# Masked chunk matrices of RWKV as row-tiled products per head, four chunks to one item and two banks

## The chip, the cores and the metric

The kernel runs on one core of one Trainium2 chip. The metric is device time of one launch in microseconds (us); less is better. Engines are named as the profile names them: PE is the matrix engine (TensorE), PEld its weight loads, DVE is VectorE, ACT is ScalarE, POOL is GpSimd, SP is SyncE, whose queue issues the transfers (DMA). PSUM is the memory that PE writes its products to, in eight banks of 512 fp32 columns; SBUF is the working memory of the other engines.

## The reference, cut to what matters

One layer of a hybrid decoder: one input projection, then a gated linear attention branch (GLA, 4 heads) and an RWKV-7 branch (16 heads of 64) beside each other, then a gated merge, an output projection and a layer norm. It runs over a prompt of 1024 tokens and over 8 single-token samples.

```python
p = jnp.einsum('btd,dn->btn', x, w_in)          # 1024 -> 9360 columns
...
def step(S, inp):                               # RWKV-7, every head, every token
    rt, wt, kt, vt, kkt, at = inp
    sa = jnp.einsum('bhvk,bhk->bhv', S, -kkt)
    S = S * wt[:, :, None, :] + sa[..., None] * (kkt * at)[:, :, None, :] + vt[..., None] * kt[:, :, None, :]
    y = jnp.einsum('bhvk,bhk->bhv', S, rt)
    return S, y
...
m = (jax.nn.sigmoid(gate_a) * jnp.einsum('btc,cd->btd', o_gla, w_up_gla)
     + jax.nn.sigmoid(gate_b) * jnp.einsum('btc,cd->btd', o_rwkv, w_up_rwkv))
out = jnp.einsum('btd,de->bte', m, w_out)
y_out = _layernorm(DEEPNORM_ALPHA * x + out, ln_g, ln_b, LN_EPS)
```

The kernel does the recurrence of RWKV in chunks of 64 tokens. Within a chunk it needs, for each head, four masked 64 by 64 matrices: the products of the two decayed key-side rows (b and k) with the two decayed query-side rows (a and r), one pair under a strict triangle and the other with its diagonal.

## The kernel before

The prompt is worked through in two passes of 512 tokens (`PASS`); the 8 samples ride along in the first. In each pass the projection runs over column blocks of 128: eight weight tiles, each as a high and a low part, give 24 products per block and stretch of tokens (`proj<-xh,wpart` and `proj<-xl,wpart` in the profile; `big` and `pY` banks are also lent to the up-projections and the output). The 16 RWKV heads are handled as eight pairs, one head on partitions 0 to 63 and the other on 64 to 127 (`HS`). For each pair the stream `pair` runs `front` (decays, keys, and the masked matrices), then the solution of the triangular systems with help of transfers through DRAM (`LD`, `XD`), then `back`, `turn`, `chain` (eight chunks one after the other, each with four small products: `pch<-wide,gg`, `pY<-az,wide`, `pch<-rh,XT`, `pch<-wide`, and `pY<-gg,wide`) and `norm`. GLA heads run as streams of their own (`gla_head`).

No one writes the order of the instructions by hand. All streams are Python generators that yield operations; `run` takes at each step the operation whose key is smallest: the start that the planner computes for it from its own prices (`price`) and hop times, less a bonus by kind of stream. Each operation that is yielded is one item and is issued at once to its engine's queue; each queue is then worked off in that order on the chip. So a price that changes or an operation that is longer moves the rest of the plan as well. Tiles of PSUM come from rings: `BANKS` gives `big` three banks, `proj` two, `pY` two and `pch` one. `get(tag, n)` waits until n buffers of a ring are idle at the same time, and other streams may take a single one meanwhile; `free` gives a buffer back.

The place of the change is the end of `front`. `BK` (the tile `wide`) holds for each chunk 128 columns, for the one head b and k, for the other k and b. `AZ` (the tile `az`) holds for each chunk 256 columns in the order kind, head, token. Its block for head 0 is filled on partitions 0 to 63 alone and that for head 1 on 64 to 127 alone; the rest is zero from the start. So one product over all 128 partitions per chunk gives both heads' matrices. Two chunks fill one bank, DVE multiplies the bank with the mask `gmask` into `gg`, and the bank is given back: four banks and four masks per pair.

Of the kernel before, what the change touches and what calls it, by code (L numbers as in the profile page):

```python
# [20 lines left out]
P = 128  # L21
D = 1024
# [10 lines left out]
C = 64  # L33
NCH = HT // C
# [52 lines left out]
HS = (slice(0, 64), slice(64, 128))  # L87
# [42 lines left out]
class Op:  # L130


    def __init__(self, ways, out, ins, lag=0.0, table=None, tiles=None, port=""):
        self.ways, self.out, self.ins, self.lag, self.table, self.tiles = ways, out, ins, lag, table, tiles
        self.port = port
        self.eng, self.fn, self.cost = ways[0]


def tiles(name, args):

    m = args[0].free_size()
    return tuple(32 if v <= 32 else 64 if v <= 64 else P for v in (args[0].shape[0], m))


def price(eng, name, out, args, ins):

    n = out.free_size()
    src = [x for x in ins if x.tensor.space != PSUM] if eng == "A" else ins
    if eng == "P":
        m = args[0].free_size()  # L150
        rows, cols = tiles(name, args)
        if name == "transpose":
            return 0.112
        if args[0].dtype == F32R:
            return max(m / 1200, n / 2165) if rows == cols == P else (m + n) / 1200
        if rows == cols == P:
            return 2 * max(m, n) / 1200 + 0.005
        return 2 * (m + n) / 1200 * rows * cols / P ** 2
    if eng == "S":
        return 0.56  # L160
    if eng == "A":
        extra = len(ins) - 1
        return 0.097 + n / 1200 + (0.042 if len(src) == len(ins) else 0.0) + 0.094 * extra
    wide = max([n, *(x.free_size() for x in ins)]) if name in ("tensor_reduce", "bn_stats", "bn_aggr") else n
    if eng == "V":
        if name == "tensor_tensor_scan":
            return 0.1 + n / 480
        if name in ("tensor_copy", "copy", "memset") and ins and ins[0].tensor.space != PSUM:
            wide = wide / 2
        scalars = sum(x.free_size() == 1 for x in ins[1:]) if name in ("scalar_tensor_tensor", "tensor_scalar") else 0  # L170
        return 0.068 + wide / 960 + 0.06 * scalars
    if name in ("tensor_scalar", "memset"):
        return 0.08 + n / 760
    return 0.1 + n / (300 if name == "tensor_copy" else 456)
# [25 lines left out]
def transfer(out, src):  # L200

    n = 4 * min(run_of(out), run_of(src), 512 if src.tensor.space == out.tensor.space else 1024)
    return out.nbytes() / n * (0.01 + n * 4.65e-5) / 16, 1.7 if out.tensor.space != DRAM else 1.2


class Engine:
# [3 lines left out]
    def __getattr__(self, name):  # L210
        def make(out, *args, **kw):
            ins = [x for x in (*args, *kw.values()) if isinstance(x, AP)]
            ways = []
            lag, table, part, port = 0.0, None, None, ""
            for eng, handle in self._handles.items():
                call = getattr(handle, "tensor_copy" if (eng, name) == ("V", "copy") else name)
                ways.append((eng, lambda call=call: call(out, *args, **kw), price(eng, name, out, args, ins)))  # L217
                if eng in "VG" and shared(eng, name, out, ins):
                    port += eng
            if eng == "S":  # L220
                lag = transfer(out, args[0])
            elif eng == "A" and name == "activation":
                table = SETS.get(args[1])
            elif eng == "P":
                part = tiles(name, args)
            return Op(ways, out, ins, lag, table, part, port)
        return make


class Stream:  # L230
# [8 lines left out]
class Order:  # L239
# [83 lines left out]
    def start(self, op):  # L323

        best = None
        for eng, fn, cost in op.ways:
            free, t = self.time[eng] + (SWITCH if eng == "P" and op.tiles != self.tiles else 0.0), 0.0
            for x in (op.out, *op.ins):
                at, by = self.ready.get(x.tensor.name, (0.0, None))
                if eng == "S" and by == "D" and x is op.out:  # L330
                    continue
                if by != eng:
                    at += HOP.get(by, 0.0) + (SPARE if eng == "P" and by in ("V", "A", "G") else LANDED if by == "D" else 0.0)
                elif eng != "P" and x is not op.out:
                    at += 0.13
                t = max(t, at)
            t = max(t, self.read.get(op.out.tensor.name, 0.0))
            if eng in op.port:
                free = max(free, self.port["G" if eng == "V" else "V"])
            late, t = free - t, max(t, free)  # L340
            if eng in "VA" and self.held(eng, op):
                cost += HOLD
            end = t + cost
            if len(op.ways) > 1:
                end += BIAS if eng == "V" and "A" in op.ways[0][0] else ASIDE if eng == "G" and "G" in op.port else 0.0
            if best is None or end < best[0]:
                best = end, t
                op.eng, op.fn, op.cost, op.late = eng, fn, cost, max(0.0, late)
        return best[1]
# [10 lines left out]
    def run(self):  # L360
        while self.streams:
            best, before = None, list(self.streams)
            self.urgent = self.needed()
            for s in before:
                self.advance(s)
                if s.op is not None:
                    t = self.start(s.op)
                    key = t - (s.on_pe if s.op.eng == "P" else s.prio)
                    if s.kind in self.urgent:
                        key -= URGENT  # L370
                    if s.op.table not in (None, self.table):
                        key += max(0.0, TABLE - AGE * s.op.late)
                    if best is None or key < best[0]:
                        best = key, t, s
            if best is None:
                assert self.streams != before, "streams wait for one another"
                continue
            _, t, s = best
            op, s.op = s.op, None
            cost = op.cost  # L380
            if op.table not in (None, self.table):
                cost += TABLE
                self.table = op.table
                self.nc.scalar.preload_act_table_set(self.table)  # L384
            op.fn()
            self.time[op.eng] = max(self.time[op.eng], t + cost)
            if op.eng in op.port:
                self.port[op.eng] = t + cost
            if op.eng == "P":
                self.tiles = op.tiles  # L390
            elif op.eng in "VA":
                for x, q in self.starts(op):
                    self.quads[op.eng][x is op.out, x.space] = q
            end = t + cost
            if op.eng == "S":
                self.dma = max(self.dma, end) + op.lag[0]
                end = self.dma + op.lag[1]
            end = max(end, self.ready.get(op.out.tensor.name, (0.0,))[0])
            self.ready[op.out.tensor.name] = end, "D" if op.eng == "S" else op.eng
            for x in op.ins:  # L400
                n = x.tensor.name
                self.read[n] = max(self.read.get(n, 0.0), end)


class Kern(Order):
# [654 lines left out]
    def front(self, c, p, st, d):  # L1060
        a, A, V, E = self.a, self.A, self.V, self.E
        BK_, L_ = yield from self.get("wide", 2)
        az, gg = (yield from self.get("az")), (yield from self.get("gg"))
        BK = BK_.rearrange("p (c t) -> p c t", c=NCH)
        AZ, GG = (x.rearrange("p (c k h t) -> p c k h t", c=NCH, k=2, h=2) for x in (az, gg))
# [26 lines left out]
        ps = yield from self.head_sums(te)  # L1092
# [23 lines left out]
        ps = yield from self.head_sums(te)  # L1116
# [4 lines left out]
        if c.fronts == NPAIR:  # L1121
            self.free(*c.lw)

        mk = self.cst("gmask").unsqueeze(1).to_broadcast([P, 2, 2 * P])
        for x in range(0, NCH, 2):
            p1 = yield from self.bank("big", [P, 2, 2 * P])
            for n in range(2):
                yield self.P.matmul(p1[:, n], BK[:, x + n], az[:, (x + n) * 2 * P:(x + n + 1) * 2 * P], start=True, stop=True)
            yield V.tensor_mul(gg[:, x * 2 * P:(x + 2) * 2 * P].rearrange("p (n t) -> p n t", n=2), p1, mk)
            self.free(p1)  # L1130

        NU = 4 * NCH
        LD = self.dr.tile([4, NCH, 32, 32], F32, name=f"LD{c.i}{p}")
# [27 lines left out]
        H = NCH // 2  # L1161
# [5 lines left out]
        for q in range(2):  # L1167
            b = slice(32 * q, 32 * q + 32)
            for h in range(2):
                n = 2 * q + h  # L1170
# [554 lines left out]
```

## Time and profile before

| what | value |
|---|---|
| median of 3 runs | 1603.45 us (1600.87 to 1605.56) |
| the profiled execution | 1597.82 us, of which the span of its instructions 1596.0 |
| PE busy in the span | 1550.1 us, 97% |
| PEld busy | 1371.0 us, 86% |
| DVE busy | 1282.5 us, 80% |
| ACT busy | 855.9 us, 54% |
| POOL busy | 123.5 us, 8% |
| mean DMA rate | 200 GB/s |
| mean granted clock of PE | 0.997 of full speed |

An fp32 product shows as two records on PE and two weight loads on PEld (the tile is loaded and run in two parts), an fp32r product as one of each. A row of grouped instructions reads: line, engine, operation, output <- inputs, rows*columns of the array that it uses, shape of the operand that moves through, count, then busy time in us and the mean duration of one in ns. Durations of records overlap, since the next product starts before the last has left the array; the pace of a series is therefore the distance of its starts, not the duration of one. In a timeline the first number is the start and the second the time from the first start to the last end of the merged rows, both in us.

### The profile page before, as it was taken

The numbers are of one execution on the slowest core, as the hardware profiler recorded it, in microseconds if no ns is written. First come the engines' busy times: TensorE is split into PE (matmuls) and PEld (weight loads), VectorE is DVE, ScalarE is ACT, GpSimd is POOL, SyncE is SP. The second block draws the span as 40 slices with busy tenths as digits, with TensorE's granted clock in tenths as the row PEclk, the third lists the DMA queues.
The fourth block names the chain that finished last, engine by engine and source line by source line (L and its number), as shares of the span: only waits on it lengthen the run. The fifth ranks groups of instructions, "written<-read, shape, count | busy, mean of one in ns | idle before, by whom it ended". The sixth has DMA issues, their size and how long they took to land.

```text
span 1596.0 us, 29099 instructions
## 1 busy us (share of the span) xinstructions
PE 1550.1 (97%) x9874; PEld 1371.0 (86%) x9874; DVE 1282.5 (80%) x3351; ACT 855.9 (54%) x2032; POOL 123.5 (8%) x218
## 2 busy tenths in 40 slices
PE   8999999999999999999999999999999999999998
PEld 6999999999999998787888777878777889988786
DVE  6697889878989798779788997899877786756565
ACT  5564666566657665553654464445454646544210
POOL 2011001100000011001101120011001000000000
PEclk9999999999999999999999999999999999999999
DMA  9767776676757765755465546544665467797332
GB/s 308 245 233 221 231 232 224 204 260 222 232 188 250 246 219 184 213 162 172 144 194 161 168 119 212 168 152 134 204 174 144 161 211 255 255 300 251 128 117 82
DMA packets 206641, 318.42 MB, mean 200 GB/s; under 512 B 87076, under 2 KB 102573, under 8 KB 206493
## 3 DMA queue, kind: packets, MB, share of 16 engines
q1 hardware_dynamic: 206492, 316.56, 62.6%
q8 instruction: 79, 1.29, 0.3%
q14 instruction: 70, 0.57, 0.1%
HBM read 196.82 MB, written 118.61 MB: 198 GB/s over the span
## 4 chain that ended last, share of the span: by engine, by line
PE 60%; DVE 23%; DMA 6%; SPq 4%; issue 4%; ACT 3%; POOL 0%; DVEq 0%; POOLq 0%; ACTq 0%
PE proj L217 30%; PE big L217 19%; DVE row L217 8%; PE pY L217 7%; PE pch L217 4%; SPq L217 4%; DVE Xt L217 3%; DVE X L217 3%; DVE wide L217 2%; DVE wpart L217 2%; DMA wide<-LD 1%; DVE az L217 1%; DMA wraw<-w_in 1%; ACT row L217 1%; DVE pair L217 1%
## 5 line engine op out<-in xcount | busy, mean ns | idle before, releaser
L217 PE MATMUL proj<-xh,wpart 128*128 128x256 f32 (+2 forms) x3744 | 915.5, 328 | 2.4 <-DMA wpart<-w 2.0
L217 PEld LDWEIGHTS proj<-xh,wpart 128*128 128x128 f32 x3744 | 624.2, 189 | 52.3 <-issue 5.1
L217 PE MATMUL proj<-xl,wpart 128*128 128x264 f32 (+2 forms) x1872 | 611.6, 327 | 0.9 <-DVE xl L217 0.7
L217 PEld LDWEIGHTS proj<-xl,wpart 128*128 128x128 f32 x1872 | 353.3, 189 | 25.4 <-issue 1.7
L217 ACT CAST wpart<-wraw 128x512 fp32r<-128x512 f32 x210 | 130.3, 623 | 113.7 <-PE proj L217 44.0
L217 DVE TENSOR_TENSOR wpart<-wraw,wpart 128x512 fp32r<-128x512 f32 x207 | 142.3, 689 | 38.1 <-ACT wpart L217 37.3
L217 DVE TENSOR_TENSOR row<-row 128x512 f32<-128x512 f32 (+10 forms) x302 | 164.0, 549 | 7.3 <-ACT row L217 2.4
L217 ACT ACTIVATE row<-row 128x512 f32<-128x512 f32 (+5 forms) x229 | 139.1, 611 | 36.0 <-DVE row L217 25.2
L217 DVE TENSOR_TENSOR Xt<-X,wide 128x60 f32<-128x60 f32 (+24 forms) x496 | 108.7, 219 | 17.9 <-DMA wide<-LD 6.8
L217 DVE TENSOR_TENSOR X<-X,Xt 128x60 f32<-128x60 f32 (+24 forms) x496 | 109.0, 220 | 12.3 <-DVE Xt L217 0.5
L217 ACT ACTIVATE s0p<-wide,pc 64x64 f32<-64x64 f32 x256 | 88.0, 344 | 46.7 <-DVE wide L217 41.0
L217 POOL TENSOR_TENSOR row<-row 128x256 f32<-128x256 f32 (+5 forms) x67 | 67.2, 1005 | 575.8 <-DVE row L217 238.6
L217 ACT ACTIVATE row<-proj,omu 128x256 f32<-128x256 f32 (+1 forms) x99 | 54.1, 547 | 98.6 <-PE proj L217 98.4
L217 PE MATMUL big<-row 128*128 128x128 f32 (+3 forms) x520 | 96.4, 287 | 9.4 <-DVE Xt L217 4.0
L217 PEld LDWEIGHTS big<-row 128*128 128x128 f32 (+1 forms) x520 | 74.8, 187 | 20.0 <-ACT row L217 11.3
L384 ACT ACT_TABLE_LOAD x66 | 84.7, 1283 | 1.1
L217 DVE SCALAR_TENSOR_TENSOR wide<-pch,pc,s0p 64x64 f32<-64x64 f32 x224 | 63.2, 282 | 22.7 <-PE pch L217 17.4
L217 DVE SCALAR_TENSOR_TENSOR row<-proj,pv,row 128x255 f32<-128x255 f32 (+1 forms) x99 | 56.2, 568 | 26.6 <-ACT tail L217 17.5
L217 PE MATMUL big<-xh,wpart 128*128 128x512 f32 (+2 forms) x304 | 74.8, 329 | 0.0
L217 ACT COPY row<-big 128x128 f32<-128x128 f32 (+5 forms) x134 | 38.5, 317 | 64.8 <-PE big L217 56.5
L217 PE MATMUL big<-az,wide 128*128 128x256 f32 x256 | 66.4, 384 | 0.4 <-DVE row L217 0.2
L217 PE MATMUL big<-part,headsr 128*128 128x512 f32 x128 | 55.7, 440 | 7.3 <-ACT part L217 3.4
(240 smaller groups left out, 2506.9 us busy)
## 6 DMA issues: line engine op xcount, KB each, us to landing
w<-wpart SPq DMA_DIRECT2D x146, 512.0 KB
wpart<-w SPq DMA_DIRECT2D x146, 512.0 KB
wraw<-w_in SPq DMA_DIRECT2D x146, 256.0 KB
wide<-LD SPq DMA_DIRECT2D x64, 128.0 KB
wraw<-w_up_gla SPq DMA_DIRECT2D x32, 256.0 KB
wraw<-w_up_rwkv SPq DMA_DIRECT2D x32, 256.0 KB
sg<-row SPq DMA_DIRECT2D x16, 260.0 KB
row<-sg SPq DMA_DIRECT2D x16, 260.0 KB
```

What stands on the lines that cost most here:

```text
L217: ways.append((eng, lambda call=call: call(out, *args, **kw), price(eng, name, out, args, ins)))
L384: self.nc.scalar.preload_act_table_set(self.table)
```

## The change

The masked matrices are no longer one product of 128 rows per chunk but two of 64 rows, one for each head, on the head's own partitions. The product of head h and chunk c has `BK[hs, c]` (64 x 128) as weights and moves `AZ[hs, c, :, h]` (64 x 2 x 64, two runs of 64 columns that lie 128 apart). The zero blocks of `az` are not read here any more (they still are in `chain`). Head 0 writes to one bank and head 1 to another, four chunks each, so that two `big` banks must be idle at once, and the eight products of four chunks are yielded as one item through the new function `together`: the planner places them next to each other and nothing can come between them. DVE's four masks per pair stay, with the same 512 columns each; they now write runs of 64. The planner's price of a product that uses 128 columns and fewer rows is changed, and so is that of DVE's predicated copy, which GLA uses.

```diff
@@ class Op
-        self.port = port
+        self.port, self.outs = port, [out]
@@ price
-        return 2 * (m + n) / 1200 * rows * cols / P ** 2
+        return 2 * (max(m, n) if cols == P else m + n) / 1200 * rows * cols / P ** 2 + (0.01 if cols == P else 0.0)
...
-        return 0.068 + wide / 960 + 0.06 * scalars
+        return 0.068 + wide / (480 if name == "copy_predicated" else 960) + 0.06 * scalars
@@ new
+def together(ops):
+
+    op = ops[0]
+    fns = [x.fn for x in ops]
+    op.ways = [(op.eng, lambda: [fn() for fn in fns], sum(x.cost for x in ops))]
+    op.ins = [y for x in ops for y in x.ins]
+    op.outs = [x.out for x in ops]
+    op.eng, op.fn, op.cost = op.ways[0]
+    return op
@@ start
-            for x in (op.out, *op.ins):
+            for x in (*op.outs, *op.ins):
...
-            t = max(t, self.read.get(op.out.tensor.name, 0.0))
+            t = max(t, *(self.read.get(x.tensor.name, 0.0) for x in op.outs))
@@ run
-            end = max(end, self.ready.get(op.out.tensor.name, (0.0,))[0])
-            self.ready[op.out.tensor.name] = end, "D" if op.eng == "S" else op.eng
+            for x in op.outs:
+                n = x.tensor.name
+                self.ready[n] = max(end, self.ready.get(n, (0.0,))[0]), "D" if op.eng == "S" else op.eng
@@ front
-        mk = self.cst("gmask").unsqueeze(1).to_broadcast([P, 2, 2 * P])
-        for x in range(0, NCH, 2):
-            p1 = yield from self.bank("big", [P, 2, 2 * P])
-            for n in range(2):
-                yield self.P.matmul(p1[:, n], BK[:, x + n], az[:, (x + n) * 2 * P:(x + n + 1) * 2 * P], start=True, stop=True)
-            yield V.tensor_mul(gg[:, x * 2 * P:(x + 2) * 2 * P].rearrange("p (n t) -> p n t", n=2), p1, mk)
-            self.free(p1)
+        H = NCH // 2
+        mk = self.cst("gmask").rearrange("p (k h t) -> p k h t", k=2, h=2)
+        for x in range(0, NCH, H):
+            ps = yield from self.get("big", 2)
+            ps = [y.rearrange("p (c k t) -> p c k t", c=H, k=2) for y in ps]
+            yield together([self.P.matmul(ps[h][:, n], BK[hs, x + n], AZ[hs, x + n, :, h], start=True, stop=True)
+                            for n in range(H) for h, hs in enumerate(HS)])
+            for h in range(2):
+                yield V.tensor_mul(GG[:, x:x + H, :, h], ps[h], mk[:, :, h].unsqueeze(1).to_broadcast([P, H, 2, C]))
+            self.free(*ps)
```

The first place is PE at the first pair of the first pass, around the masked matrices (`big<-az,wide`). `proj<-` rows are the projection, `big<-part,headsr` are sums over a head, `big<-row 8x512` belongs to the samples. Before:

```order
L217 MATMUL proj<-xh_235,wpart 128x256
L217 MATMUL big<-part,headsr 128x512
L217 MATMUL big<-az_167,wide 128x256 x8
L217 MATMUL big<-row 8x512
L217 MATMUL proj<-xl_273,wpart 128x256
```

And now:

```order
L217 MATMUL proj<-xh_265,wpart 128x256
L217 MATMUL big<-az_167,wide 128x128 x8
L217 MATMUL big<-row 8x512
L217 MATMUL proj<-xl_277,wpart 128x256
L217 MATMUL proj<-xh_265,wpart 128x256
L217 MATMUL proj<-xh_270,wpart 128x256
L217 MATMUL proj<-xl_298,wpart 128x256
L217 MATMUL proj<-xh_270,wpart 128x256
L217 MATMUL big<-az_167,wide 128x128 x8
L217 MATMUL proj<-xh_191,wpart 128x264
```

The eight products in one row become two items of eight, with one product of the samples and five of the projection between them.

The second place is PE at the third pair, where the chain of the pair before it (`pch` and `pY` rows) and a GLA head (`big<-row 128x1`) run beside the masked matrices. Before:

```order
L217 MATMUL pY<-az_168,wide 128x128
L217 MATMUL big<-part,headsr 128x512
L217 MATMUL proj<-xh_258,wpart 128x256
L217 MATMUL big<-az_167,wide 128x256 x2
L217 MATMUL pch<-rh,XT_172 128x128
L217 MATMUL big<-az_167,wide 128x256 x2
L217 MATMUL big<-row 128x1
L217 MATMUL big<-az_167,wide 128x256
L217 MATMUL pch<-wide 128x128
L217 MATMUL big<-az_167,wide 128x256 x3
L217 MATMUL pY<-gg,wide 128x128
```

And now:

```order
L217 MATMUL pY<-az_168,wide 128x128
L217 MATMUL big<-az_167,wide 128x128 x8
L217 MATMUL pch<-rh,XT_172 128x128
L217 MATMUL big<-row 128x1 x2
L217 MATMUL proj<-xh_223,wpart 128x256
L217 MATMUL proj<-xh_227,wpart 128x256
L217 MATMUL proj<-xl_242,wpart 128x256
L217 MATMUL proj<-xh_227,wpart 128x256
L217 MATMUL proj<-xh_235,wpart 128x256
L217 MATMUL proj<-xl_273,wpart 128x256
L217 MATMUL big<-az_167,wide 128x128 x8
L217 MATMUL pch<-wide 128x128
```

Steps of the chain stood between the masked products; now they stand before and after an item of eight. In the whole plan there are 32 such items, and at least one product of 128 rows stands between any two of them.

The third place is DVE at the same pair, where it takes the banks out through the mask (`gg<-big,cons`). `rh<-pch` and `wide<-pch,pc,s0p` are steps of the chain, `row` is GLA and the front. Before:

```order
L217 COPY rh<-pch 128x128
L217 TENSOR_SCALAR row<-row 128x256
L217 TENSOR_TENSOR row<-big,row 128x512
L217 TENSOR_TENSOR gg<-big,cons 128x512
L217 TENSOR_SCALAR row<-row,pv 128x512
L217 TENSOR_TENSOR gg<-big,cons 128x512
L217 TENSOR_SCALAR wide<-pch,pc,s0p 64x64 x2
L217 TENSOR_TENSOR gg<-big,cons 128x512 x2
```

And now:

```order
L217 COPY rh<-pch 128x128
L217 TENSOR_SCALAR row<-row 128x256
L217 TENSOR_SCALAR row<-row,pv 128x512
L217 TENSOR_TENSOR gg<-big,cons 128x8x64 x2
L217 TENSOR_SCALAR row<-row,pv 128x512
L217 TENSOR_SCALAR row<-row 128x256
L217 TENSOR_TENSOR gg<-big,cons 128x8x64
L217 TENSOR_SCALAR wide<-pch,pc,s0p 64x64 x2
L217 TENSOR_TENSOR gg<-big,cons 128x8x64
```

Four masks stay four; two of them now follow one item.

## The prediction

> **What bounds the kernel now.** I read the page first: busy times, the slices, and the shares of the chain of waits.
>
> ```profile
> span 1596.0 us, 29099 instructions
> ...
> PE 1550.1 (97%) x9874; PEld 1371.0 (86%) x9874; DVE 1282.5 (80%) x3351; ACT 855.9 (54%) x2032; POOL 123.5 (8%) x218
> ...
> PE   8999999999999999999999999999999999999998
> PEld 6999999999999998787888777878777889988786
> DVE  6697889878989798779788997899877786756565
> ...
> PE 60%; DVE 23%; DMA 6%; SPq 4%; issue 4%; ACT 3%; POOL 0%; DVEq 0%; POOLq 0%; ACTq 0%
> ```
>
> PE is full in nearly every slice and has 60% of the chain that ended last. That alone doesn't say that it works at its pace, since records overlap; so I looked at stages, and then at single products. The pairs, to which the change belongs, run from about 60 to 1260 us.
>
> ```profile
> 60.00:600.00 540.00, 531.57 (x4208) 515.32 (x4208) 469.24 (x1323) 341.35 (x888) 42.92 (x85) 1.00 0.71 230
> 600.00:1300.00 700.00, 677.75 (x3651) 562.20 (x3650) 589.33 (x1621) 368.12 (x849) 69.74 (x113) 1.00 0.56 170
> ```
>
> This view by stretches has span, then PE, PEld, DVE, ACT and POOL busy with their counts, then the granted clock (full in both). PE is busy for 98% of the first pass (531.57 of 540) and 97% of the second (677.75 of 700). DVE follows with 87% and 84%: second in line, so that a gain on PE needn't come through whole.
>
> **The products that go.** The answers for the tiles `az` and `gg`, and the timeline of the first pair:
>
> ```profile
> L217 PE MATMUL big<-az,wide x256: 377/379/483, 60.1 to 1259.2; 128*128 128x256 f32 x128
> L217 DVE TENSOR_TENSOR az<-row x61: 673/685/1737, 47.9 to 1247.2; 64x512 f32<-64x512 f32 x61
> ...
>   DVE gg L217: 7.4, 23
> ...
> L217 DVE TENSOR_TENSOR gg<-big,cons x64: 677/692/694, 61.1 to 1259.7; 128x512 f32<-128x512 f32 x64
> ```
>
> ```profile
> 59.82 3.45 PEld L217 LDWEIGHTS big<-az,wide 128*128 128x128 f32 x16
> 60.05 3.62 PE L217 MATMUL big<-az,wide 128*128 128x256 f32 x16
> ...
> 61.12 0.69 DVE L217 TENSOR_TENSOR gg<-big,cons 128x512 f32<-128x512 f32 x1 [0.17 <-PE big L217]
> ```
>
> Sixteen records of 256 columns take 3.62 us; without the duration of the last (0.38) that is 3.24 over 15 steps, 0.216 us a step. A pair has 16 records, so 16 x 0.216 = 3.46 us, and 16 pairs 55.3 us of PE. All of that goes.
>
> **The products that come.** A pair gets 16 products of 64 rows, 32 records of 128 columns, and half of 0.216 is 0.108 us for one. If two head tiles run side by side, 32 records make 16 steps of 0.108, 1.73 us a pair, and 16 pairs 27.6: PE saves 27.7 us. If they run one after the other, 32 x 0.108 is 3.46 and nothing is saved. No product with two row tiles stands in this trace. The nearest are the products of `wa`, which use 16 columns of the array each, in three tiles:
>
> ```profile
> 11.54 0.28 PE L217 MATMUL proj<-xh,wpart 128*128 128x256 f32 x1
> 11.75 1.06 PE L217 MATMUL big<-row,wa 128*16 128x256 f32 x12
> 12.74 0.39 PE L217 MATMUL proj<-xh,wpart 128*128 128x256 f32 x1
> 12.97 0.28 PE L217 MATMUL proj<-xl,wpart 128*128 128x256 f32 x1
> 13.09 0.28 PE L217 MATMUL proj<-xh,wpart 128*128 128x256 f32 x1
> ...
> 11.74 0.57 PEld L217 LDWEIGHTS big<-row,wa 128*16 128x16 f32 x12
> 12.74 0.19 PEld L217 LDWEIGHTS proj<-xh,wpart 128*128 128x128 f32 x1 [0.42 <-issue]
> ```
>
> Twelve fp32 records of about 256 columns would need 12 x 0.216 = 2.59 us in series. They take 0.99 (11.75 to 12.74), four rounds of three. So tiles of the array do run at the same time, here tiles side by side in columns; I take that for rows too.
>
> The weight loads could spoil it. They have a pace of their own:
>
> ```profile
> L217 PE MATMUL big<-Xt,L 128*128 128x32 f32 x128 | 16.6, 271 | 2.4 <-DVE Xt L217 1.7 <-ACT wpart L217 0.6
> L217 PE MATMUL big<-XT,As 128*128 128x64 f32 x128 | 16.4, 268 | 0.0
> ```
>
> Each pair has one series of eight such records. For 64 columns that is 16.4 / 16 = 1.03 us, less the last record's 0.27, over 7 steps: 0.108. For 32 columns it comes to 0.109. Half the columns aren't faster, so a load of 128 weight columns takes 0.108 a time. The new products need 32 loads instead of 16. Side by side they fit under the 16 steps; in a row they need 32 x 0.108 = 3.46 us again, the same bound as above. The Trainium skill ("TensorE: Matmul & The Clock Gate", LDWEIGHTS) speaks for the second: it says that a load costs by its columns and not by its rows, so that a half-high tile loads no faster. By that alone the change would save nothing; the same skill ("TensorEngine Tiling (Array Packing)", Key Properties) says that different tiles may load and multiply in parallel, and no run here shows either of it for row tiles. What the trace has is twelve loads of `wa` under four rounds; 16-column loads are too short to settle it. I take the parallel case as likeliest.
>
> **What a change of tiling costs.** Each item of eight is entered from a product with 128 rows and left to one: 32 times in and out. The price stands around the one kind of product with 64 rows, that of the samples:
>
> ```profile
> 46.16 0.28 PE L217 MATMUL proj<-xl,wpart 128*128 128x256 f32 x1
> 46.27 0.28 PE L217 MATMUL proj<-xh,wpart 128*128 128x256 f32 x1
> 46.48 1.02 PE L217 MATMUL big<-row 64*8 64x512 f32 x2
> 47.43 0.39 PE L217 MATMUL proj<-xh,wpart 128*128 128x256 f32 x1
> 47.66 0.28 PE L217 MATMUL proj<-xl,wpart 128*128 128x256 f32 x1
> 47.78 0.40 PE L217 MATMUL proj<-xh,wpart 128*128 128x256 f32 x2
> ```
>
> In: 0.21 us from 46.27 to 46.48, where projection products are 0.12 apart (47.66 to 47.78): 0.09. The two records of 512 columns should take 2 x 0.432 = 0.86 and take 0.95 (46.48 to 47.43): 0.09. Out: 0.23 to the next product, 0.11 over the usual. That makes 0.29. On entry to the new item 128 weight columns must be loaded uncovered, where the samples' tile has 8: another 0.108, as on the way out. Together 0.39 an item, and 32 items 12.5 us. The lower bound is 0.29, or 9.3 us, if the first load is covered.
>
> **The rest of the change.** DVE's masks stay 64 of 692 ns: the writes in runs of 64 have a like in `az<-row`, which writes the same pattern with 512 columns in 685. The banks of an item come full together, 8 x 0.108 + 0.2 = 1.1 us after PE turns to it, and DVE empties them in 2 x 0.69. Until then only one `big` bank is left, and the second item waits. The order puts about 0.95 (the samples' product) and five projection products of 0.12 there at the first pair, 1.55 us against 1.38 plus a hop of 0.17, so PE is covered; uncovered, one mask would be 0.69 on PE. The steps of the chain that stood between the old products now wait for up to one item, 1.25 us instead of 0.43, twice a pair; projection work behind them on PE hides that. The other prices move the plan everywhere: by the order 18 more instructions go to POOL, which at 8% busy has room. I cost this at nothing, give or take 8 us: a quarter of the 30.7 us for which PE isn't busy in the two stretches (8.4 and 22.3). The quarter is a choice; what a new order gains or loses must come out of such gaps, and the trace of before can't show where.
>
> **Sum.** 27.7 - 12.5 = 15.2 us less on PE. The stretches in which DVE has the chain (23% against 60%) don't shrink with PE, so I let four fifths through: 12 us. The profiled execution (1597.82, the span and 1.8 around it) would come to 1586; its time lies 5.6 below the median of the runs, and against that median, 1603.45, the forecast is 1591.
>
> **Rivals.** First, the row tiles do not overlap, by loads or by products. Then nothing is saved and the price of the tiling stays: 12.5 us slower, 1616. For it: two loads at once with 128 columns aren't seen anywhere. Against it: three tiles ran at once above. This is also what the skill's rule on loads would give.
>
> Second, the two banks become a wait. If PE stands still for one mask at each item (0.69 x 32 = 22 us), that takes more than the 15.2 saved: 7 us slower, 1610. It decides from 0.48 us an item (15.2 / 32). For it: three `big` banks, and DVE at 87%, so a mask may stand behind other work in DVE's queue. Against it: the row `DVE gg` above says that DVE waited for the products, 7.4 us in 23 waits, so the masks were mostly ready to take a bank when it was full, and projection work stands between items. In a milder form, with half of that stall, it ends at 1599, no change.
>
> Third, DVE is the bound once PE is quicker: half of the gain comes through, 7 us, 1596. For it the 87%; against it the gap to PE's 98%.
>
> **How the numbers follow.** The measurement tells about 0.3% from no change, 4.8 us either way. Forecast with overlap 0.55 (own range 1577 to 1599: from 27.7 less 9.3 with the plan's 8 on top, 26 us, to 12 less 8, 4 us), no overlap 0.20, the wait on banks 0.15, DVE 0.10. Faster takes 0.50 of the first, 0.06 of DVE and 0.02 of the wait: 0.58. Same takes 0.04, 0.04, 0.05 and 0.02 of no overlap: 0.15. Slower: 0.01, 0.08 and 0.18: 0.27. The range runs from 1576, which would be the whole 27.7 with nothing paid for the tiling, to 1616, the price of no overlap: it leaves about 0.1 above and 0.06 below.
>
> **What would show it.** Right: the items of 16 records take about 0.9 to 1.1 us from first to last start with starts in twos, the fp32 records of `big<-az` fall to about half of their 66 us busy, and PE's next product comes some 0.2 late. Wrong: starts 0.108 apart throughout (no overlap); `PE big` or its loads waiting for `DVE gg` (banks); DVE over 90% with PE idle (DVE). It falls as a whole if the masked products are quick and the span still doesn't move: then the new order has lost elsewhere what they gained.

## The result and the profile after

| | before | changed |
|---|---|---|
| median | 1603.93 us (4 runs, 1600.87 to 1605.56) | 1582.35 us (4 runs, 1581.66 to 1582.96) |
| span of the profiled execution | 1596.0 us | 1579.6 us |

The ratio is 0.9868, with a 95% interval of 0.985 to 0.9885: 21.6 us faster by the medians, 18 to 24 by the interval. The two spans are only 16.4 us apart, since the profiled execution of before was one of its quickest: its granted clock was 0.997, where most runs of before beside the experiments have 0.992 to 0.996. Those runs scatter from 1595 us (at 0.999) to 1612 us (at 0.993).

The page of the changed kernel, the rows that answer to those of before:

```profile
span 1579.6 us, 29594 instructions
...
PE 1535.2 (97%) x10130; PEld 1357.4 (86%) x10130; DVE 1281.5 (81%) x3355; ACT 843.9 (53%) x2004; POOL 151.0 (10%) x236
...
PE 67%; DVE 19%; DMA 6%; issue 3%; ACT 2%; SPq 2%; POOL 0%; DVEq 0%; POOLq 0%; ACTq 0%
```

PE is busy for 14.9 us less (1550.1 before), and still 97% of a shorter span. Its share of the chain that ended last has grown from 60 to 67%, and that of DVE has fallen from 23 to 19%. The same two stretches as before, and the tile `az` (loads and products with min, median and max in ns, then what the engines waited for ahead of it, then who waited for it):

```profile
60.00:600.00 540.00, 532.03 (x4382) 516.95 (x4380) 467.66 (x1323) 347.44 (x899) 57.81 (x95) 0.99 0.72 234
600.00:1300.00 700.00, 680.05 (x3883) 563.68 (x3883) 600.33 (x1639) 360.31 (x831) 82.34 (x122) 1.00 0.56 172
```

```profile
L217 PEld LDWEIGHTS big<-az,wide x512: 182/188/188, 60.7 to 1246.0; 64*128 64x128 f32 x171
L217 PE MATMUL big<-az,wide x512: 272/272/374, 60.7 to 1246.1; 64*128 64x128 f32 x171
...
  DVE gg L217: 0.7, 2
...
  DVE gg L217: 6.4, 10
```

DVE is at 87% and 86%, so it did not become the bound. Ahead of this tile's instructions only 0.7 us of idle time ended with a mask (`gg`), in two waits: no queue has formed at the two banks. One item, in the timeline of the changed kernel at the first pair:

```profile
60.34 0.39 PE L217 MATMUL proj<-xh,wpart 128*128 128x256 f32 x2
60.66 0.97 PEld L217 LDWEIGHTS big<-az,wide 64*128 64x128 f32 x16
60.67 1.16 PE L217 MATMUL big<-az,wide 64*128 64x128 f32 x16
61.76 0.09 PEld L217 LDWEIGHTS big<-row 64*8 64x8 f32 x2
61.76 1.02 PE L217 MATMUL big<-row 64*8 64x512 f32 x2
61.86 1.29 DVE L217 TENSOR_TENSOR gg<-big,cons 128x512 f32<-128x512 f32 x2 [1.10 <-PE big L217]
```

Sixteen records take 1.16 us; without the last record's 0.27 that is 0.89 from first to last start. In series, 15 steps of 0.108 would be 1.62. In the records of this item the two heads start 6 to 7 ns apart and each pair 0.111 to 0.112 us after the one before it, but the first step takes 0.21 (the same is to be seen in rows of their own in the last experiment): the second weight load of each tile starts 0.11 us after the first, and the second record 0.11 us after that load. From the first start to the next product, 60.67 to 61.76, the item occupies 1.09 us. So do 23 of the 32 items; in the other nine the second head starts late, and they occupy up to 1.57 us. The longest, out of the timeline:

```profile
436.98 0.68 DVE L217 TENSOR_TENSOR row<-big,row 128x512 f32<-128x512 f32 x1
...
437.23 1.64 PE L217 MATMUL big<-az,wide 64*128 64x128 f32 x16
...
437.72 0.96 PEld L217 LDWEIGHTS big<-az,wide 64*128 64x128 f32 x14 [0.19 <-DVE row L217]
```

The load of the second head waits until DVE has read another `big` tile out, at 437.66; that looks like a wait for the second bank. The mean of all items is 1.14 us, so such waits cost 32 x 0.05 = 1.5 us in all.

### The profile page after: what moved, and what is told of

The parts are those of the page before. It is cut to its first block, busy times and chain, and to the rows that moved or that the text cites. A ratio compares the mean times of both kernels' runs of the same rounds, so it can differ in the third digit from the quotient of the medians.

```text
span 1579.6 us, 29594 instructions
## 1 busy us (share of the span) xinstructions
PE 1535.2 (97%) x10130; PEld 1357.4 (86%) x10130; DVE 1281.5 (81%) x3355; ACT 843.9 (53%) x2004; POOL 151.0 (10%) x236
## 4 chain that ended last, share of the span: by engine, by line
PE 67%; DVE 19%; DMA 6%; issue 3%; ACT 2%; SPq 2%; POOL 0%; DVEq 0%; POOLq 0%; ACTq 0%
PE proj L217 38%; PE big L217 19%; PE pY L217 6%; DVE row L217 6%; PE pch L217 4%; DVE Xt L217 4%; DVE X L217 3%; DVE wide L217 2%; SPq L217 2%; ACT row L217 1%; DVE wpart L217 1%; DMA wide<-LD 1%; DVE pair L217 1%; DMA row<-o_rwkv 1%; DMA row<-sg 1%
## 5 line engine op out<-in xcount | busy, mean ns | idle before, releaser
L217 PE MATMUL proj<-xh,wpart 128*128 128x256 f32 (+2 forms) x3760 | 925.2, 329 | 3.1 <-DMA wpart<-w 3.0
L217 PE MATMUL proj<-xl,wpart 128*128 128x256 f32 (+2 forms) x1880 | 614.8, 327 | 0.0
L217 ACT ACTIVATE row<-row 128x512 f32<-128x512 f32 (+4 forms) x229 | 138.8, 611 | 45.3 <-DVE row L217 31.4
L217 DVE TENSOR_TENSOR row<-row 128x512 f32<-128x512 f32 (+9 forms) x284 | 150.0, 535 | 4.6 <-ACT row L217 0.6
L217 POOL TENSOR_TENSOR row<-row 128x256 f32<-128x256 f32 (+5 forms) x85 | 89.2, 1054 | 658.4 <-DVE row L217 335.4
L217 DVE TENSOR_TENSOR Xt<-X,wide 128x60 f32<-128x60 f32 (+24 forms) x496 | 112.0, 226 | 21.7 <-DMA wide<-LD 10.7
L217 ACT COPY row<-big 128x128 f32<-128x128 f32 (+6 forms) x137 | 38.5, 311 | 65.0 <-PE big L217 60.5
L217 DVE SCALAR_TENSOR_TENSOR row<-proj,pv,row 128x255 f32<-128x255 f32 (+1 forms) x99 | 56.3, 569 | 17.5 <-ACT tail L217 10.3
L217 PE MATMUL big<-xh,wpart 128*128 128x512 f32 (+2 forms) x272 | 68.3, 333 | 1.2 <-ACT xh L217 1.2
L217 ACT COPY wide<-pch 64x64 f32<-64x64 f32 x134 | 27.6, 206 | 64.4 <-PE pch L217 42.4
```

## The experiments

They ran in three groups, each beside runs of the kernel before, whose medians are 1603.15 us (the first four), 1602.8 (the next four) and 1605.79 (the last four).

**The new price alone.** Before, with the planner's new price of a predicated copy:

```diff
-        return 0.068 + wide / 960 + 0.06 * scalars
+        return 0.068 + wide / (480 if name == "copy_predicated" else 960) + 0.06 * scalars
```

> The kernel before with one edit: the planner's doubled price of a predicated copy. The products stay 128 rows high. Theory (the gain of 21.6 us by the medians is 15 us of array time, 0.47 us at each of 32 items, and the rest is the new plan): 0 to 7 us faster than before, ratio 0.9955 to 1.000. Rival (the new plan made most of it, the tiling little): 12 us or more faster, ratio below 0.9925, at an unchanged 55 us of masked products.

Measured: 1607.81 us, ratio 1.0023 (1.0004 to 1.0041). Neither side had it: the price by itself makes a plan that is a little slower. It moves work to POOL as the change does (147.9 us busy there, 123.5 before), so that shift alone brings no gain.

**Row tiles with the old price.** The change, with the diff above undone.

> The change without the new price of a predicated copy: row tiles and items of eight stay. Theory: 15 us from the array with the old plan's accidents, 10 to 22 us faster than before, ratio 0.986 to 0.994. Rival (the price made it): within 5 us of before, ratio 0.997 to 1.003.

Measured: 1588.47 us, ratio 0.990 (0.9877 to 0.9923), 14.7 us faster than the 1603.15 beside it. The theory holds; the price isn't needed for most of the gain.

**Grouping alone.** The change, but with the old products, four of 128 rows to an item:

```diff
-            yield together([self.P.matmul(ps[h][:, n], BK[hs, x + n], AZ[hs, x + n, :, h], start=True, stop=True)
-                            for n in range(H) for h, hs in enumerate(HS)])
+            yield together([self.P.matmul(ps[n // 2][:, n % 2], BK[:, x + n], az[:, (x + n) * 2 * P:(x + n + 1) * 2 * P], start=True, stop=True)
+                            for n in range(H)])
```

(The masks take whole banks again.)

> The change with the old products: four products of 128 rows and 256 columns as one item to two banks, all prices of the change kept. Array time is that of before, 3.46 us a pair. Theory: no gain from grouping alone, ratio 0.996 to 1.004. Rival (grouping and the plan that follows from it is the gain): ratio below 0.992. If holding two banks costs a wait, 5 us or more slower.

Measured: 1604.08 us, ratio 1.0006 (0.9989 to 1.0022). Two banks for one item cost nothing and bring nothing that this interval shows; neither does the plan that the planner makes around such items. Its products cost what they did; their group in the table of products reads

```profile
L217 PE MATMUL big<-az,wide 128*128 128x256 f32 x256 | 60.9, 381 | 0.2 <-DVE gg L217 0.2
```

where before has 66.4 us busy and the change has 38.7 (the last fences of this document).

**The heads one after the other.** The change with the same plan to the last instruction but for the order inside the item:

```diff
-                            for n in range(H) for h, hs in enumerate(HS)])
+                            for h, hs in enumerate(HS) for n in range(H)])
```

> The change with one edit inside the item: first the four products of head 0, then the four of head 1; plan and prices are the same. Theory (only neighbours in the queue on different row tiles overlap): 16 records 0.108 apart, an item takes 1.73 instead of 0.89 us from first to last start, 32 x 0.84 = 27 us slower than the change and some 5 us slower than before, ratio 1.000 to 1.008. Rival (PE takes later products of the other tile ahead, so that the order doesn't matter): as the change, ratio 0.985 to 0.989.

Measured: 1595.64 us, ratio 0.9956 (0.9937 to 0.9975): 13.3 us slower than the change, and 7 us faster than before. Both the theory and the rival are off. Its first item in the timeline:

```profile
61.44 0.39 PE L217 MATMUL proj<-xh,wpart 128*128 128x256 f32 x2
61.76 1.71 PE L217 MATMUL big<-az,wide 64*128 64x128 f32 x16
63.40 1.02 PE L217 MATMUL big<-row 64*8 64x512 f32 x2
```

The item occupies 1.64 us where the change has 1.09. From first to last start it is 1.71 - 0.27 = 1.44 us, neither the 1.62 of a series nor 0.89. The records show why: head 1 starts when five of head 0's eight records have started, 0.55 us into the item, and runs beside the other three. So PE looks ahead, but only a few products. The page of this run begins

```profile
PE 1551.7 (97%) x10130; PEld 1374.9 (86%) x10130; DVE 1284.5 (80%) x3355; ACT 843.2 (53%) x2004; POOL 149.6 (9%) x236
```

The run does two more things. It gives the price of PE time in an unchanged plan. 32 x 0.55 would be 17.6 us more on PE; the page has 16.5 (1551.7 against 1535.2), since nine items of the change are longer than 1.09 us. That made 13.3 us by the medians, four fifths. The intervals of the two ratios leave anything from 10 to 18 us, and the two profiled executions lie 16.8 us apart, which is all of it. And it shows that not all of the gain is array time: its items cost PE 1.64 us plus about 0.2 for the ways in and out, 1.84 instead of the 1.73 of the old products, 3.5 us more in 32 items, and by the medians it is still 7 us faster than before (4 to 10 by the interval).

**No grouping.** Every row-tiled product is an item of its own:

```diff
-            yield together([self.P.matmul(ps[h][:, n], BK[hs, x + n], AZ[hs, x + n, :, h], start=True, stop=True)
-                            for n in range(H) for h, hs in enumerate(HS)])
+            for n in range(H):
+                for h, hs in enumerate(HS):
+                    yield self.P.matmul(ps[h][:, n], BK[hs, x + n], AZ[hs, x + n, :, h], start=True, stop=True)
```

> The change without the grouping: each row-tiled product is an item of its own, all else as in the change. In its plan 13 of the 32 groups are split into one and seven products by other work, so 45 groups stand where 32 stood. Theory (each further way into and out of the tiling costs 0.39 us): 13 x 0.39 = 5 us slower than the change, ratio to before 0.987 to 0.994. Rival (the planner puts single items where they wait less, and that is worth more): as fast as the change or faster, ratio 0.987 or less.

Measured: 1595.59 us, ratio 0.9956 (0.9942 to 0.9969), 13.2 us slower than the change. The direction is the theory's, the size is larger. The first split group and its rest in the timeline:

```profile
60.55 0.40 PE L217 MATMUL big<-part,headsr 128*128 128x512 f32 x1
60.88 0.49 PE L217 MATMUL big<-az,wide 64*128 64x128 f32 x2
61.29 0.38 PE L217 MATMUL proj<-xl,wpart 128*128 128x256 f32 x1
61.51 0.40 PE L217 MATMUL proj<-xh,wpart 128*128 128x256 f32 x2
61.75 0.28 PE L217 MATMUL proj<-xl,wpart 128*128 128x256 f32 x1
61.96 1.16 PE L217 MATMUL big<-az,wide 64*128 64x128 f32 x14
63.04 1.02 PE L217 MATMUL big<-row 64*8 64x512 f32 x2
```

One product by itself has nothing to overlap with and holds PE for 0.41 us (60.88 to 61.29), and its partner's absence makes the other seven last as long as eight: 1.16 for 14 records, as for 16. With the way in (0.09) and the slow start after it (61.29 to 61.51 is 0.22, 0.10 too much) a split costs 0.6 us, 13 of them 7.8. The 19 groups that stay whole are longer too: they occupy 1.25 us on average, up to 1.83, where the items of the change have 1.14, because in ten of them the second head starts late. That adds 2 us. The page agrees, with PE busy for 10.3 us more than in the change:

```profile
PE 1545.5 (97%) x10130; PEld 1361.4 (85%) x10130; DVE 1272.1 (80%) x3336; ACT 851.4 (53%) x2018; POOL 146.7 (9%) x241
```

Of the 13.2 us that leaves about 3 to the plan. What the late heads wait for is not shown.

**Other plans with and without row tiles.** To see what a plan does by accident, one of the planner's other prices was moved a little, in the change and in the kernel before: `HOLD` from 0.11 to 0.12 and `ASIDE` from 0.5 to 0.45. Neither touches a product. A further run put 0.2 us more into the planner's price of an item.

> The change with one of the planner's other prices moved a little (HOLD 0.12 for 0.11), which touches no product: a plan that differs by accident. Theory (15 of the 21.6 us are the array's, some 6 are luck of this plan): 2 to 10 us slower than the change, ratio 0.988 to 0.993. Rival (the 6 us belong to the change, and every plan with it has them): within 2 us of the change, ratio 0.985 to 0.988.

> The kernel before with the same little move (HOLD 0.12 for 0.11). Theory (plans differ by luck by about 5 us either way): ratio 0.996 to 1.004. Rival (the plan of before was an unlucky one, by 6 us): ratio 0.994 to 0.997.

> The change with 0.2 us more in the planner's price of an item of eight, which brings it from 1.03 with its switch nearer to the 1.25 us that PE spends. Theory (the plan is better where its prices are true): 0 to 5 us faster than the change, ratio 0.983 to 0.987. Rival (any other price only draws another plan): anywhere within 6 us of the change, ratio 0.985 to 0.992.

> The change with another of the planner's prices moved a little (ASIDE 0.45 for 0.5): another plan by accident. Theory (15 us from the array, give or take 6 by the plan): ratio 0.986 to 0.995, around 0.990. Rival (the change's own 0.987 is what such plans give): 0.985 to 0.988.

> The kernel before with the same little move (ASIDE 0.45 for 0.5). Theory: ratio 0.996 to 1.004. Rival (before is an unlucky plan): 0.994 to 0.997.

> The changed kernel once more, on the chip of the runs beside it. Theory (its own plan is lucky by some 6 us, and that repeats): ratio 0.985 to 0.989. Rival (its first measurement was a matter of the chip): ratio 0.989 to 0.992, like the three other plans with row tiles.

| plan | row tiles | ratio to before | interval |
|---|---|---|---|
| the change | yes | 0.9868 | 0.985 to 0.9885 |
| the change again | yes | 0.9872 | 0.9852 to 0.9892 |
| change, ASIDE 0.45 | yes | 0.9872 | 0.9852 to 0.9891 |
| change, HOLD 0.12 | yes | 0.9897 | 0.988 to 0.9914 |
| change, item price + 0.2 | yes | 0.9897 | 0.988 to 0.9913 |
| change, old copy price | yes | 0.990 | 0.9877 to 0.9923 |
| before, HOLD 0.12 | no | 0.9993 | 0.9977 to 1.0009 |
| before, ASIDE 0.45 | no | 1.0017 | 0.9997 to 1.0038 |
| before, new copy price | no | 1.0023 | 1.0004 to 1.0041 |
| grouped, 128 rows | no | 1.0006 | 0.9989 to 1.0022 |

The change's number repeats beside other runs of before, as its theory had it. Its plan is among the better ones with row tiles, but not alone: the one with ASIDE 0.45 is as good by accident, as its rival had it; three are some 5 us behind, with intervals that touch. The truer price of an item made no better plan, as its rival had it. Without row tiles no plan stands out, and before wasn't an unlucky one.

**Sixteen products to an item.** To halve the ways in and out, all of a pair in one item, with one bank of `pY` and all three of `big`:

```diff
-        for x in range(0, NCH, H):
-            ps = yield from self.get("big", 2)
...
+        raw = [(yield from self.get("pY")), *(yield from self.get("big", 3))]
+        ps = [y.rearrange("p (c k t) -> p c k t", c=H, k=2) for y in raw]
+        yield together([self.P.matmul(ps[2 * (n // H) + h][:, n % H], BK[hs, n], AZ[hs, n, :, h], start=True, stop=True)
+                        for n in range(NCH) for h, hs in enumerate(HS)])
```

> The change with all sixteen products of a pair as one item, to three banks of big and one of pY: 16 ways into and out of the tiling instead of 32. Theory (0.39 us of array time for each): 6 us less on PE, 0.98 to 0.986, if the banks cost nothing. Rival (four of five banks at once make the streams wait for each other): slower than the change by 5 us or more, ratio 0.99 to 1.01.

Measured: 1606.92 us, ratio 1.0011 (0.9998 to 1.0024): all of the gain is lost. An item does what it should, and since its two tiles have different names here, the timeline keeps their records apart:

```profile
63.11 0.37 PE L217 MATMUL pY<-az,wide 64*128 64x128 f32 x1
63.12 0.37 PE L217 MATMUL big<-az,wide 64*128 64x128 f32 x1
63.33 0.27 PE L217 MATMUL pY<-az,wide 64*128 64x128 f32 x1
63.33 0.27 PE L217 MATMUL big<-az,wide 64*128 64x128 f32 x1
63.44 0.27 PE L217 MATMUL pY<-az,wide 64*128 64x128 f32 x1
63.44 0.27 PE L217 MATMUL big<-az,wide 64*128 64x128 f32 x1
...
65.10 0.51 PE L217 MATMUL proj<-xh,wpart 128*128 128x264 f32 x2
```

The records start in twos, one of each head, 0.21 us apart at first and then 0.11; the 32 take 1.99 us to the next product, against 2 x 1.09 and a second way in and out. But PE stands still elsewhere (the view by stretches, and the longest wait of PE):

```profile
60.00:600.00 540.00, 516.66 (x4200) 500.83 (x4199) 445.48 (x1264) 325.09 (x869) 37.05 (x71) 0.97 0.69 224
...
PE big L217 <- DVE Xt L217: 11.9, 6, 7.0
```

In the first pass PE is idle for 23.3 of 540 us; in the change it is 8.0. DVE has less done in the same stretch too (445.48 us against 467.66). The streams are late: the masked products of the second pair begin at 147 us, in the change at 127, and the first of the second pass at 667 instead of 618. That they wait for a time at which all four banks are free fits this, but no row shows that wait by itself; on a mask directly PE waited once, 1.7 us. The granted clock falls to 0.97 in that stretch, where the change has 0.99, and over the whole run it is 0.982 to 0.987 in all twelve runs, 0.992 to 0.999 in the runs of before beside them. With it PE is busy for 8.5 us more than in the change (1543.7 against 1535.2), although the items need less; how much of the loss is the clock's was not separated.

None of these versions beats the changed kernel; the best beside it ties with it.

## Why the prediction was right, and what was mis-sized

The forecast was 1591 us, 12 us faster, and the range 1576 to 1616; the time is 1582. The direction, the mechanism and every term of the array's account held, nearly to the size:

- **The stream.** Two row tiles do run side by side. 16 steps of 0.108 a pair were forecast; the trace has 0.112, and 0.21 for the first step of each item. The step from tiles side by side in columns (the products of `wa`) to tiles in rows, which no row of before could prove, was right.
- **The weight loads** overlap too: 32 loads a pair fit under 16 steps. So the Trainium skill's rule that a load costs by its columns ("TensorE: Matmul & The Clock Gate", LDWEIGHTS) is not contradicted: a record of a load of 64 rows lasts 188 ns, one of 128 rows 190 ns. But the loads of two tiles don't add up. What the Trainium skill says of tiles that load in parallel ("TensorEngine Tiling (Array Packing)", Key Properties) agrees with this trace: loads of the two heads start 7 ns apart.
- **The price of the tiling.** 0.39 us an item was forecast. The item costs 0.09 on entry, occupies 1.09, and makes the next product 0.11 late: 1.29 us, of which 8 x 0.112 = 0.89 is the stream, so 0.40. The 0.10 of the uncovered first load is there, as the step of 0.21 inside the item. Array time saved: (1.73 - 1.29) x 32 = 14.1 us, or 12.5 with the mean of 1.14 for all items; forecast 15.2.
- **What comes through.** Four fifths were assumed. Heads in turn, the same plan with 16.5 us more PE time, gives 13.3 / 16.5, four fifths by the medians, and all of it by the profiled executions. So the array's part of the gain is 10 to 14 us, and the forecast for that part was 12.
- **DVE's masks**: 692 ns before, 688 after, as said.

The term that was mis-sized is the new order, which the prediction put at nothing, give or take 8 us. The gain is 21.6 us (18 to 24) and the array's part 10 to 14, so the change's own plan brought some 8 to 12 us by the medians. That is not a remainder alone: heads in turn, which has that plan and spends 3.5 us more on its items than before, is 7 us faster. So the sign was wrongly taken as even; that the bound of 8 us was too tight is likely, but not clear of the noise. The step behind the bound failed more plainly: "what a new order gains or loses must come out of such gaps". In the two profiled executions the time in which PE is not busy is 45.9 us before and 44.4 in the change; only 1.5 us came out of gaps. The kept profiles of all these plans say the same, at a mean granted clock of 0.993 on both sides: the six with row tiles (the change twice, two prices moved, the item price, the old copy price) have PE busy for 1535 to 1538 us and not busy for 44 to 48; the five without (before, two prices moved, the new copy price, grouping alone) have 1550 to 1559 and 46 to 55. By the means that is 18.9 us less in PE's busy time and 3.1 less in its gaps. The items account for 12.5 to 14 of the 18.9; in which products the other 5 were saved stays open.

Of the plans with row tiles all gain more than the array's part (16 to 21 us by their ratios), and of those without none is faster than before by more than its interval; so the order seems to gain when the masked products are short. Why, the runs don't settle: neither the grouping, nor the new price of the copy, nor the work on POOL gave a gain when it was had alone. DVE's share of the chain is 23% before and 19% in the change, but the price alone, which is slower, has the same 19%:

```profile
PE 70%; DVE 19%; DMA 4%; ACT 2%; issue 2%; SPq 1%; POOL 0%; POOLq 0%; DVEq 0%; ACTq 0%
```

(This is the chain of the kernel with the new price alone.) So that share explains nothing.

The rivals: no overlap is refuted by the starts in twos. The wait on banks is refuted for two but for a small rest (grouping alone 1.0006; 0.7 us of idle time ahead of the tile, 1.5 us in late second heads), and the loss with four fits it without proving it. DVE as the bound is refuted by its 87 and 86% and by the four fifths or more of PE time that come through.

## What to carry to other kernels

Where a product is block-diagonal with zeros, two row tiles with a bank each nearly halve its stream, if neighbours in the queue lie on different tiles; the way into the tiling and out costs 0.4 us here, so products should be issued in groups that are worth several times that, and not in groups that need nearly all banks at once: here the larger group, with four banks, lost the whole gain. A gain in a planned kernel must be judged over several plans: here the same edit was worth 16 to 21 us, by the plan that came with it.

## What the runs showed of the hardware

- Alternate heads overlap at once, heads in turn only from the fifth of eight records on: 0.55 us into the item. PE starts products of the other tile ahead of the rest of the first one's, over about three records and not over a whole item. Across row tiles the queue is therefore not worked off strictly in its order.
- One half-high product by itself (two records) holds PE for 0.41 us before the next can start, more than a third of the 1.09 us that eight hold it for.
- In the version with four banks the granted clock fell to 0.97 over a stretch in which PE was idle for 23 us; in the change it was 0.99 with 8 us. Which of the two led to the other is not shown.

The numbers of the group that the text above refers to, from the tables of products, before and in the changed kernel:

```profile
L217 PE MATMUL big<-az,wide 128*128 128x256 f32 x256 | 66.4, 384 | 0.4 <-DVE row L217 0.2
L217 PE MATMUL big<-az,wide 64*128 64x128 f32 x512 | 38.7, 285 | 0.0
```

The time in which at least one record of the group runs falls from 66.4 to 38.7 us, to 58%, of which the tails at each of the 32 items are a part.
